# Encoder trunk, opening of layer 0: inputs handed over transposed, norm weight multiplied into the split, root of the mean square applied behind the products

## The chip, the cores and the metric

The kernel runs on one core of one Trainium2 chip. The core has engines that run side by side, each working through its own list in order: TensorE (PE in the profile, with PEld for its weight loads), VectorE (DVE), ScalarE (ACT), GpSimd (POOL) and SyncE (SP, which issues most of the transfers). The metric is the device time of one execution in microseconds (us), lower is better; what counts is the median of several runs.

## The reference, cut to what matters

The program is a two-layer encoder on one sequence of 1024 tokens of width 1024, with 256 memory tokens. Layer 0 has windowed attention, layer 1 a gated linear recurrence; each also has four cross-attention heads into the memory, and ends with a convolutional feed-forward part. What matters here is the opening:

```python
def rmsnorm(x, g):
    y = xf * lax.rsqrt(jnp.mean(xf * xf, axis=-1, keepdims=True) + NORM_EPS)
    return (y * g.astype(F32)).astype(x.dtype)
...
mem_n = rmsnorm(mem, mem_norm_g)
h = x
for layer in range(DEPTH):
    u = rmsnorm(h, norm_g[layer, 0])
    mem_kv = mem_n @ w_mem_kv[layer]
    y = mixer_window_attn(u, mem_kv, a_w_in[slot], ...)    # layer 0
    ...
# in mixer_window_attn
q, k, v, xq = jnp.split(u @ w_in, ...)
q, k = rope(q), rope(k)
s = jnp.einsum(xq, memory keys) * X_HEAD_DIM ** -0.5       # cross-attention
```

A norm is thus a factor for each token (the root) and a factor for each channel (the weight g). The root of a token goes through a product unchanged, since it scales a whole row of the product's input; g does not.

## The kernel before, in words

Products run in three passes on PE for accuracy (`mm3`, lines 80 to 83): each operand is split into a high part `h` in a shortened format and a rest `l`, and high x high, low x high and high x low are added up in one PSUM bank. The split of a tile is two operations: ACT casts `h` (line 86, or line 76 for a weight unit), DVE subtracts for `l` (line 87 or 77). A weight unit (`wunit`, lines 69 to 78) is one transfer by SP into one of four stage buffers, then this split into one of four ring buffers.

`start()` (line 1367) makes the normed, transposed and split inputs. `rows` (line 1374) loads a block of 128 tokens, `norm_T` (lines 107 to 118) sums its squares on ACT (line 100), makes the mean on DVE (line 91), takes the power -0.5 on POOL (line 93: one column, since a token's root is one number for each partition), multiplies by root and weight on DVE (line 112), turns it by eight transposes on PE (line 116) and splits what comes out of PSUM. Two blocks of the memory become `mh`, `ml`; eight blocks of x become `uh`, `ul`.

`memory_kv` (lines 148 to 176) runs right behind the two memory blocks. For each of two layers it makes four key blocks (`km`: 24 products 128x256 each, weights as the stationary side, so that memory tokens lie along the columns) and two value blocks (`vm`: 48 products 128x512, memory tokens on the partitions), and sends them to memory (`kvd`). Key and value blocks all take a bank from one PSUM pool of four (`psb`, tag `pb`). After each key block and each value unit, `step` takes up one more block of x, so the norm of x runs between the products of the memory.

`window()` (line 227) follows: `proj` (line 252) makes query, key and value of a group of heads (24 products 128x384 into a bank `pj`), turns queries and keys by the tables `cos` and `sin` (lines 274 and 275), adds on POOL (276, 277) and splits the values (279, 280). `cross_unit` (line 185) does the cross-attention with the largest score, a scale and an exponential (lines 204 to 209).

The lists of the engines are made by a scheduler ahead of time: it simulates the program with its own costs and writes down for each engine the order in which it got to the instructions. So an edit in the opening can change the order everywhere behind it. Waits between engines are semaphores; an engine whose next instruction waits does nothing else meanwhile.

Of the kernel before, what the change touches and what calls it, by code (L numbers as in the profile page):

```python
# [27 lines left out]
RING = 4  # L28
STAGE = 4

MEM_POOL = 1
QKV_POOL = (0, 2, 2, 2)

XU = [(0, 2), (0, 2), (2, 2), (0, 0)]
# [12 lines left out]
def build(tc, A, out):  # L47
# [12 lines left out]
    up = tc.alloc_tile_pool(name="uT", bufs=1)  # L60

    ident = cp.tile([P, P], F32, name="ident")
    nc.sync.dma_start(ident, A["ident"])
# [81 lines left out]

    kvd = [dram.tile([4, P, 2, 256], F32, name=f"kvd{l}") for l in range(2)]

    def memory_kv(tp, psb, mh, ml, step):

        for l in range(2):  # L150
            km = tp.tile([P, 4, 256], F32, tag="km", bufs=1, name="km")
            vm = tp.tile([P, 2, 512], F32, tag="vm", bufs=1, name="vm")
            for h in range(4):
                wh, wl = wunit(A["wmk"][l, h], eng=pool if 4 * l + h < MEM_POOL else None)
                ps = psb.tile([P, 512], F32, tag="pb", name="pb")
                for k in range(KT):
                    c = slice(k * P, (k + 1) * P)
                    mm3(ps[:, :256], wh[:, c], wl[:, c], mh[:, k, :], ml[:, k, :], k == 0, k == KT - 1)
                act.copy(km[:, h, :], ps[:, :256])
                step()  # L160
            pv = [psb.tile([P, 512], F32, tag="pb", name="pb") for _ in range(2)]
            for u in range(4):
                wh, wl = wunit(A["wmv"][l, u])
                for i in range(2):
                    k = 2 * u + i
                    c = slice(i * 512, (i + 1) * 512)
                    for t in range(2):
                        m = slice(t * P, (t + 1) * P)
                        mm3(pv[t], mh[:, k, m], ml[:, k, m], wh[:, c], wl[:, c], k == 0, k == KT - 1)
                step()  # L170
            for t in range(2):
# [13 lines left out]
    def cross_unit(l, h, b, head, wp, tags, w0, pair):  # L185

        wh, wl, kvh, kvl = head
        ps = tags["pj"][2].tile([P, 512], F32, tag=tags["pj"][0], bufs=tags["pj"][1], name="pj")
        for k in range(KT):
            c = slice(k * P, (k + 1) * P)  # L190
            m = slice(b * 512, (b + 1) * 512)
            mm3(ps, wh[:, c], wl[:, c], uh[:, k, m], ul[:, k, m], k == 0, k == KT - 1)
        xh, xl = pair("x", b)
        with tc.high_priority(AHEAD):
            split(xh, xl, ps)
        p = wp.tile([P, 4, 256], F32, tag="sm", bufs=tags["sm"], name="xp")
# [25 lines left out]
        ot = w0.tile([P, 512], F32, tag=tags.get("xo", "xo"), bufs=1, name="xo")  # L222
        act.copy(ot, po)
        act.dma_start(oT[l][8 + h, :, b * 512:(b + 1) * 512], ot)


    def window():
# [24 lines left out]
        def proj(g):  # L252
# [6 lines left out]
            for b in range(2):  # L259
                rqs = []  # L260
                for tt in range(4):
                    t = 4 * b + tt
                    ps = psq.tile([P, 384], F32, tag="pj", bufs=2, name="pj")
                    for k in range(KT):
                        wh, wl = us[k // 2]
                        c = slice((k % 2) * 384, (k % 2 + 1) * 384)
                        m = slice(t * P, (t + 1) * P)
                        mm3(ps, uh[:, k, m], ul[:, k, m], wh[:, c], wl[:, c], k == 0, k == KT - 1)
                    t1 = ea.tile([P, 320], F32, tag="t1", bufs=1, name="t1")
                    t2 = ea.tile([P, 320], F32, tag="t2", bufs=1, name="t2")  # L270
# [12 lines left out]
                for w in range(3):  # L283
# [1080 lines left out]
        return late  # L1364


    def start():
        psp = tc.alloc_tile_pool(name="mps", bufs=2, space=PSUM, reuse_waits="tile")
        psb = tc.alloc_tile_pool(name="mpb", bufs=4, space=PSUM, reuse_waits="tile")
        tp = tc.alloc_tile_pool(name="mt", bufs=2, reuse_waits="tile")  # L1370
        mh = tp.tile([P, KT, 256], F32R, bufs=1, name="mh")
        ml = tp.tile([P, KT, 256], F32R, bufs=1, name="ml")

        def rows(src, t, g, dh, dl):
            x = tp.tile([P, D], F32, tag="x", bufs=4, name="x")
            nc.sync.dma_start(x, src[t * P:(t + 1) * P, :])
            if not g:
                g.append(grow(tp, *g_src.pop(0)))
            norm_T(tp, psp, x, g[0], dh, dl, t)

        g_src = [(A["mem_norm_g"], "gm"), (A["norm_g"][0, 0:1, :], "g0")]
        gm, g0 = [], []
        for t in range(2):
            rows(A["mem"], t, gm, mh, ml)
        left = list(range(NT))

        def step():
            if left:
                rows(A["x"], left.pop(0), g0, uh, ul)

        memory_kv(tp, psb, mh, ml, step)
        tp.release()
        psb.release()
        psp.release()
# [5 lines left out]
    wo0.finish()  # L1400
    ffn(0, wo0, h2d, True, (0, 1), (0, 1))
    late = hgrn()
    wo1.finish()
# [6 lines left out]
def prepare(i):  # L1410
# [8 lines left out]

    a = {}  # L1420
    a["x"] = c(f["x"].reshape(T, D))
    a["mem"] = c(f["mem"].reshape(256, D))
    a["norm_g"] = c(f["norm_g"])
    a["mem_norm_g"] = c(f["mem_norm_g"].reshape(1, D))
# [64 lines left out]
```

## Time and profile before

| | |
|---|---|
| median of 3 runs | 2690.17 us (2688.71 to 2694.20) |
| profiled execution | 2686.47 us, its span 2684.7 us |
| mean granted clock of TensorE | 0.993 |
| first and last product of the memory | 13.99 and 67.54 us |
| first product of `proj` | 67.77 us |
| output projection of layer 0, first sum on DVE | 495.4 us |

The span runs from the first to the last instruction; 1.8 us of the execution lie outside it. A row of instructions in the profile reads: line, engine, operation, tile written and tiles read, shape, count, then the busy time and the mean of one in ns, the idle time ahead of them and who ended it. Buffer numbers are left out of the names there. Matmuls overlap on PE, so their durations add up to more than they take; the distance between two starts is what one costs.

### The profile page before, as it was taken

The numbers are of one execution on the slowest core, as the hardware profiler recorded it, in microseconds if no ns is written. First come the engines' busy times: TensorE is split into PE (matmuls) and PEld (weight loads), VectorE is DVE, ScalarE is ACT, GpSimd is POOL, SyncE is SP. The second block draws the span as 40 slices with busy tenths as digits, with TensorE's granted clock in tenths as the row PEclk, the third lists the DMA queues.
The fourth block names the chain that finished last, engine by engine and source line by source line (L and its number), as shares of the span: only waits on it lengthen the run. The fifth ranks groups of instructions, "written<-read, shape, count | busy, mean of one in ns | idle before, by whom it ended". The sixth has DMA issues, their size and how long they took to land.

```text
span 2684.7 us, 39333 instructions
## 1 busy us (share of the span) xinstructions
PE 2618.3 (98%) x14496; PEld 2200.0 (82%) x14496; DVE 1827.6 (68%) x3026; ACT 1384.6 (52%) x2530; POOL 469.4 (17%) x520
## 2 busy tenths in 40 slices
PE   8999999999999999999999999999999999999998
PEld 7888897788888887887888888888888788888886
DVE  6587787678656565478778686796757755656456
ACT  6367666645444445455455454545534444444453
POOL 1231110111111100032223132230211111110013
PEclk9999998999999999999999999999999999999999
DMA  7674213557877756674326252102436777774666
GB/s 281 213 166 104 60 28 117 176 183 181 216 199 200 205 165 243 191 241 157 103 84 177 76 120 70 48 29 83 150 119 178 183 202 210 198 205 160 220 196 228
DMA packets 204626, 427.00 MB, mean 159 GB/s; under 512 B 20112, under 2 KB 66576, under 8 KB 198800
## 3 DMA queue, kind: packets, MB, share of 16 engines
q1 hardware_dynamic: 171168, 326.68, 37.5%
q0 software_dynamic: 24544, 90.19, 16.1%
q10 hardware_dynamic: 8720, 7.60, 0.9%
q8 instruction: 114, 1.87, 0.3%
q14 instruction: 80, 0.66, 0.1%
HBM read 331.08 MB, written 117.44 MB: 167 GB/s over the span
## 4 chain that ended last, share of the span: by engine, by line
PE 77%; DVE 13%; ACT 4%; DMA 3%; issue 2%; POOL 1%; SPq 0%; DVEq 0%; ACTq 0%; POOLq 0%
PE X L638 27%; PE V L638 11%; PE pj L81 5%; PE pj L82 5%; PE Y L638 5%; PE pj L83 5%; PE pb L82 3%; PE pb L81 3%; PE pb L83 3%; DVE E L1194 1%; DVE ER L1229 1%; PE pt L338 1%; PE pt L116 1%; DVE wl L87 1%; PE po L1297 1%
## 5 line engine op out<-in xcount | busy, mean ns | idle before, releaser
L87 DVE TENSOR_TENSOR wl<-st,wh 128x1024 fp32r<-128x1024 f32 (+1 forms) x238 | 263.5, 1114 | 325.7 <-ACT wh L86 318.3
L86 ACT CAST wh<-st 128x1024 fp32r<-128x1024 f32 (+1 forms) x238 | 222.5, 937 | 295.2 <-PE X L638 196.2
L81 PE MATMUL pj<-uh,wh 128*128 128x512 f32 x512 | 204.1, 399 | 3.8 <-DVE xl L87 2.5
L638 PE MATMUL X<-wl,wh 128*128 128x512 f32 x528 | 204.8, 390 | 0.3 <-DVE wl L87 0.3
L638 PE MATMUL X<-wh,wl 128*128 128x512 f32 x528 | 204.6, 389 | 0.0
L82 PE MATMUL pj<-ul,wh 128*128 128x512 f32 x512 | 202.5, 396 | 0.1
L83 PE MATMUL pj<-uh,wl 128*128 128x512 f32 x512 | 201.6, 394 | 0.0
L638 PE MATMUL X<-wh 128*128 128x512 f32 x528 | 198.8, 390 | 1.7 <-DVE c L1014 0.9
L81 PE MATMUL pj<-wh,uh 128*128 128x384 f32 (+1 forms) x512 | 190.4, 372 | 4.2 <-DVE gs L1125 3.8
L82 PE MATMUL pj<-wl,uh 128*128 128x384 f32 (+1 forms) x512 | 187.3, 366 | 0.0
L83 PE MATMUL pj<-wh,ul 128*128 128x384 f32 (+1 forms) x512 | 186.8, 366 | 0.0
L77 DVE TENSOR_TENSOR wl<-st,wh 128x1024 fp32r<-128x1024 f32 (+1 forms) x92 | 119.9, 1310 | 28.1 <-ACT wh L76 27.4
L638 PE MATMUL V<-uh,wh 128*128 128x512 f32 x344 | 133.8, 389 | 0.0
L638 PE MATMUL V<-ul,wh 128*128 128x512 f32 x344 | 133.8, 389 | 0.0
L638 PE MATMUL V<-uh,wl 128*128 128x512 f32 x344 | 133.8, 389 | 0.0
L76 ACT CAST wh<-st 128x1024 fp32r<-128x1024 f32 (+1 forms) x99 | 99.9, 1015 | 50.5 <-PE pj L82 27.8
L638 PEld LDWEIGHTS X<-wh 128*128 128x128 f32 x528 | 99.1, 188 | 22.9 <-issue 1.3
L81 PEld LDWEIGHTS pj<-uh,wh 128*128 128x128 f32 x512 | 96.7, 189 | 24.2 <-DVE xl L87 2.9
L638 PEld LDWEIGHTS X<-wl,wh 128*128 128x128 f32 x528 | 99.1, 188 | 21.2 <-DVE wl L87 0.7
L638 PEld LDWEIGHTS X<-wh,wl 128*128 128x128 f32 x528 | 99.1, 188 | 20.8
L83 PEld LDWEIGHTS pj<-uh,wl 128*128 128x128 f32 x512 | 96.8, 189 | 19.2
L980 POOL TENSOR_TENSOR c<-c,g 128x512 f32<-128x512 f32 x24 | 43.4, 1828 | 393.8 <-PE X L638 162.8
(372 smaller groups left out, 7257.4 us busy)
## 6 DMA issues: line engine op xcount, KB each, us to landing
st<-hid SPq DMA_DIRECT2D x154, 256.0 KB, 3.1
st<-in_ffw_dram SPq DMA_DIRECT2D x108, 256.0 KB, 3.2
w2s<-in_ffw_dram POOLq DMA_DIRECT2D x24, 1024.0 KB, 7.9
st<-in_ffw_dram SPq DMA_DIRECT2D x46, 512.0 KB, 4.1
hid<-tt SPq DMA_DIRECT2D x88, 256.0 KB, 4.6
st<-w2s SPq DMA_DIRECT2D x88, 256.0 KB, 2.8
sx<-in_ffw_dram SPq DMA_DIRECT2D x84, 256.0 KB, 3.9
sy<-in_ffw_dram SPq DMA_DIRECT2D x42, 512.0 KB, 6.2
```

The source lines that it names most:

```text
L76: act.copy(h[:, :n], raw)
L77: (eng or dve).tensor_tensor(l[:, :n], raw, h[:, :n].bitcast(F32), op=ALU.subtract)
L81: pe.matmul(o, ah, bh, start=first, stop=False)
L82: pe.matmul(o, ah, bl, start=False, stop=False)
L83: pe.matmul(o, al, bh, start=False, stop=last)
L86: act.copy(h, src)
L87: dve.tensor_tensor(l, src, h.bitcast(F32), op=ALU.subtract)
L116: pe.transpose(ps[:, k, :], u[:, (4 * b + k) * P:(4 * b + k + 1) * P], ident)
L338: pe.transpose(tp[:, j, :], sm[:, j, c * P:(c + 1) * P], ident)
L638: pe.matmul(o, x, y, start=new, stop=e, skip_group_check=not first)
L980: pool.tensor_tensor(y[q][:, t, :], y[q][:, t, :], g3[:, c], op=ALU.mult)
L1194: dve.tensor_tensor_scan(B[:, rev], smask, a_[:, rev], 0.0, op0=ALU.mult, op1=ALU.add)
```

## The change

The host hands over x and mem already transposed (`xT`, `memT`) and the two norm weights turned so that a channel's weight lies on the channel's partition (`gT`). The kernel no longer transposes. With channels on partitions the weight is a factor for each partition, so ACT's cast takes it as its scale, and DVE's subtraction multiplies by it too (`scaled`). The root stays out of the split operands and is applied behind the products:

- memory keys: the eviction of a key block becomes a multiplication on DVE by `rsb`, the roots of the 256 memory tokens laid out on every partition;
- memory values: the eviction takes `rsm`, a token's root on its partition, as a scale;
- queries and keys of layer 0: the tables `cos` and `sin` are multiplied by `rs0`; values take it as a scale, both in the cast and in the subtraction;
- cross-attention of layer 0: the scale of the exponential and of the largest score become `xsc`, the root times the old constant.

The squares are summed over channels, which now lie on partitions, so PE does it by products with a tile of ones. For `rsb` ACT squares the memory, POOL adds the eight slices down to one, a product with ones gives the sum on every partition, DVE makes the mean, and POOL takes the power of a tile of 128x256. For x, ACT squares each slab and POOL adds it to `acc`; eight products with ones at the end give `rs0`. The first weight unit's subtraction moves from POOL to DVE, memT is loaded by ACT's queue, and `ident` is loaded later. The pool `x0`, which holds `rs0` and `xsc`, stays until the output projection is done.

```diff
-MEM_POOL = 1
...
-    def memory_kv(tp, psb, mh, ml, step):
+    def memory_kv(tp, psb, mh, ml, rsb, rsm, begin, step):
...
-                wh, wl = wunit(A["wmk"][l, h], eng=pool if 4 * l + h < MEM_POOL else None)
+                wh, wl = wunit(A["wmk"][l, h])
...
-                act.copy(km[:, h, :], ps[:, :256])
+                if l == h == 0:
+                    begin()
+                dve.tensor_tensor(km[:, h, :], ps[:, :256], rsb, op=ALU.mult)
                 step()
...
-                act.copy(vm[:, t, :], pv[t])
+                act.activation(vm[:, t, :], pv[t], AF.Copy, scale=rsm[:, t:t + 1])
...
-            dve.tensor_scalar_mul(st["nm"][:, e], st["nm"][:, e], -XSCALE)
+            if l == 0:
+                dve.tensor_tensor(st["nm"][:, e], st["nm"][:, e], xsc[:, 1, 4 * b + 2 * i:4 * b + 2 * i + 2], op=ALU.mult)
...
-                               scale=XSCALE, accum_out=st["su"][:, q:q + 1])
+                               scale=xsc[:, 0, 4 * b + q:4 * b + q + 1] if l == 0 else XSCALE, accum_out=st["su"][:, q:q + 1])
...
+        dve.tensor_tensor(cos, cos, bc(rs0.unsqueeze(2), [P, NT, 32]), op=ALU.mult)
+        s2 = sin.rearrange("p t a b -> p t (a b)")
+        dve.tensor_tensor(s2, s2, bc(rs0.unsqueeze(2), [P, NT, 64]), op=ALU.mult)
...
-                    act.copy(v[:, t, :64], ps[:, 320:])
-                    dve.tensor_tensor(v[:, t, 64:], ps[:, 320:], v[:, t, :64].bitcast(F32), op=ALU.subtract)
+                    act.activation(v[:, t, :64], ps[:, 320:], AF.Copy, scale=rs0[:, t:t + 1])
+                    dve.scalar_tensor_tensor(v[:, t, 64:], ps[:, 320:], rs0[:, t:t + 1], v[:, t, :64].bitcast(F32),
+                                             op0=ALU.mult, op1=ALU.subtract)
...
     def start():
...
+        for k in range(0, KT, 2):
+            act.dma_start(mT[:, k:k + 2], A["memT"][:, k:k + 2])
+
+        def scaled(h, l, raw, g):
+            act.activation(h, raw, AF.Identity, scale=g)
+            dve.scalar_tensor_tensor(l, raw, g, h.bitcast(F32), op0=ALU.mult, op1=ALU.subtract)
+
+        for k in range(KT):
+            scaled(mh[:, k], ml[:, k], mT[:, k], gT[:, 0, k:k + 1])
...
+        def memory_rstd():
+            for k in (0, 4):
+                act.activation(msq[:, k:k + 4], mT[:, k:k + 4], AF.Square)
+            for n in (4, 2, 1):
+                pool.tensor_tensor(msq[:, :n], msq[:, :n], msq[:, n:2 * n], op=ALU.add)
+            pb = pss.tile([P, 256], F32, name="pbc")
+            pe.matmul(pb, ones, msq[:, 0], start=True, stop=True)
+            ms = tp.tile([P, 256], F32, name="mms")
+            dve.tensor_scalar(ms, pb, 1.0 / D, EPS, op0=ALU.mult, op1=ALU.add)
+            with tc.high_priority(AHEAD):
+                pool.tensor_tensor(rsb, ms, bc(nhalf[:, 0:1], [P, 256]), op=ALU.pow)
+            pc = pss.tile([P, 2], F32, name="pcc")
...
         def step():
...
+            raw = tp.tile([P, T], F32, tag="x", bufs=4, name="x")
+            nc.sync.dma_start(raw, A["xT"][k])
+            scaled(uh[:, k], ul[:, k], raw, gT[:, 1, k:k + 1])
+            if k == 0:
+                act.activation(acc, raw, AF.Square)
+            else:
+                sq = tp.tile([P, T], F32, tag="sq", bufs=2, name="sq")
+                act.activation(sq, raw, AF.Square)
+                pool.tensor_tensor(acc, acc, sq, op=ALU.add)
...
+        for t in range(NT):
+            pe.matmul(pt[:, t:t + 1], acc[:, t * P:(t + 1) * P], ones[:, 0:1], start=True, stop=True)
+        ms = tp.tile([P, NT], F32, name="xms")
+        dve.tensor_scalar(ms, pt, 1.0 / D, EPS, op0=ALU.mult, op1=ALU.add)
+        pool.tensor_tensor(rs0, ms, nhalf, op=ALU.pow)
+        dve.tensor_scalar_mul(xsc[:, 0], rs0, XSCALE)
+        dve.tensor_scalar_mul(xsc[:, 1], rs0, -XSCALE)
```

The edit also moves instructions on every engine. Three places matter; the rows are the engines' lists as the scheduler wrote them, with buffer numbers. First PE, where the last of the first four key blocks ends and the first value blocks begin (`pb_323` and `pb_253` are the fourth key block, `pb_373`, `pb_374` and `pb_286`, `pb_287` the value blocks). Before:

```order
L81 MATMUL pb_323<-mh_93,wh_317 128x256
L82 MATMUL pb_323<-ml_94,wh_317 128x256
L83 MATMUL pb_323<-mh_93,wl_318 128x256
L81 MATMUL pb_373<-wh_375,mh_93 128x512
L81 MATMUL pb_374<-wh_375,mh_93 128x512
L82 MATMUL pb_373<-wl_376,mh_93 128x512
```

And now:

```order
L1409 MATMUL pbc_166<-msq_124,ones_99 128x256
L1416 MATMUL pcc_171<-ones_99,msq_124 128x1 x2
L80 MATMUL pb_253<-ml_103,wh_247 128x256
L81 MATMUL pb_253<-mh_102,wl_248 128x256
L79 MATMUL pb_253<-mh_102,wh_247 128x256
L80 MATMUL pb_253<-ml_103,wh_247 128x256
L81 MATMUL pb_253<-mh_102,wl_248 128x256
L79 MATMUL pb_286<-wh_288,mh_102 128x512
L80 MATMUL pb_286<-wl_289,mh_102 128x512
L81 MATMUL pb_286<-wh_288,ml_103 128x512
```

The products with ones stand inside the fourth key block, and the value blocks still follow it; they take the fifth and sixth bank of a pool of four.

Second the evictions of the key blocks, which free those banks (`km`). Before, on ACT, they stood each among the work that follows its block (`nu` is a block of x squared, `uh` its cast, `wh` a weight unit's cast):

```order
L159 COPY km_145<-pb_211 128x256
L76 CAST wh_375<-st_377 128x1024
L86 CAST uh_78<-pt_247 128x4x128
L159 COPY km_145<-pb_267 128x256
L86 CAST uh_78<-pt_254 128x4x128
L100 ACTIVATE nu_352,nss_351<-x_349 128x1024
```

Now they are on DVE:

```order
L1411 TENSOR_SCALAR mms_168<-pbc_166 128x256
L1418 TENSOR_SCALAR mm2_174<-pcc_171 128x2
L1394 SCALAR_TENSOR_TENSOR ul_78<-x_331,gT_97,uh_77 128x1024
L75 TENSOR_TENSOR wl_289<-st_290,wh_288 128x1024
L75 TENSOR_TENSOR wl_314<-st_315,wh_313 128x1024
L75 TENSOR_TENSOR wl_339<-st_340,wh_338 128x1024
L1394 SCALAR_TENSOR_TENSOR ul_78<-x_356,gT_97,uh_77 128x1024
L75 TENSOR_TENSOR wl_364<-st_365,wh_363 128x1024
L1394 SCALAR_TENSOR_TENSOR ul_78<-x_381,gT_97,uh_77 128x1024
L1394 SCALAR_TENSOR_TENSOR ul_78<-x_427,gT_97,uh_77 128x1024
L1394 SCALAR_TENSOR_TENSOR ul_78<-x_466,gT_97,uh_77 128x1024
L159 TENSOR_TENSOR km_128<-pb_136,rsb_125 128x256
```

The first eviction stands behind four weight subtractions and five slab splits that come after the mean `mms`, and three more evictions follow it in a row.

Third POOL, where `rsb` is made. Before, its list in the opening held the powers of one column and one weight subtraction:

```order
L93 TENSOR_TENSOR nrs_104<-nms_102,nhalf_76 128x1
L93 TENSOR_TENSOR nrs_128<-nms_126,nhalf_76 128x1
L77 TENSOR_TENSOR wl_148<-st_149,wh_147 128x1024
L93 TENSOR_TENSOR nrs_188<-nms_186,nhalf_76 128x1
L93 TENSOR_TENSOR nrs_244<-nms_242,nhalf_76 128x1
```

Now:

```order
L1407 TENSOR_TENSOR msq_124<-msq_124 128x1024
L1407 TENSOR_TENSOR msq_124<-msq_124 128x512
L1407 TENSOR_TENSOR msq_124<-msq_124 128x256
L1436 TENSOR_TENSOR acc_127<-acc_127,sq_283 128x1024
L1436 TENSOR_TENSOR acc_127<-acc_127,sq_310 128x1024
L1413 TENSOR_TENSOR rsb_125<-mms_168,nhalf_75 128x256
L1419 TENSOR_TENSOR rsm_126<-mm2_174,nhalf_75 128x2
L1436 TENSOR_TENSOR acc_127<-acc_127,sq_335 128x1024
L1436 TENSOR_TENSOR acc_127<-acc_127,sq_360 128x1024
```

Ten powers of one column are gone; the power for `rsb` has 256 columns and stands behind two of the seven additions to `acc`, with five behind it.

More of the change, by code (lines that the diff above doesn't have):

```diff
@@ L62, in build @@
     ident = cp.tile([P, P], F32, name="ident")
-    nc.sync.dma_start(ident, A["ident"])
     nhalf = cp.tile([P, 8], F32, name="nhalf")
@@ L204, in cross_unit @@
             dve.reduce_max(st["nm"][:, e], s, axis=AX.X)
-            dve.tensor_scalar_mul(st["nm"][:, e], st["nm"][:, e], -XSCALE)
+            if l == 0:
+                dve.tensor_tensor(st["nm"][:, e], st["nm"][:, e], xsc[:, 1, 4 * b + 2 * i:4 * b + 2 * i + 2], op=ALU.mult)
+            else:
+                dve.tensor_scalar_mul(st["nm"][:, e], st["nm"][:, e], -XSCALE)
             for j in range(2):
@@ L1364, in hgrn @@
         return late
+    x0 = tc.alloc_tile_pool(name="x0", bufs=1, reuse_waits="tile")
+    rs0 = x0.tile([P, NT], F32, name="rs0")
+    xsc = x0.tile([P, 2, NT], F32, name="xsc")
     def start():
-        psp = tc.alloc_tile_pool(name="mps", bufs=2, space=PSUM, reuse_waits="tile")
+        pss = tc.alloc_tile_pool(name="mps", bufs=1, space=PSUM, reuse_waits="tile")
         psb = tc.alloc_tile_pool(name="mpb", bufs=4, space=PSUM, reuse_waits="tile")
-        tp = tc.alloc_tile_pool(name="mt", bufs=2, reuse_waits="tile")
@@ L1371, in start @@
[L1371 to L1382, printed above, removed]
@@ L1383, in start @@
-        for t in range(2):
-            rows(A["mem"], t, gm, mh, ml)
-        left = list(range(NT))
-        def step():
-            if left:
-                rows(A["x"], left.pop(0), g0, uh, ul)
-        memory_kv(tp, psb, mh, ml, step)
+        tp = tc.alloc_tile_pool(name="mt", bufs=1, reuse_waits="tile")
+        gT = tp.tile([P, 2, KT], F32, name="gT")
+        nc.sync.dma_start(gT, A["gT"])
+        ones = tp.tile([P, P], F32, name="ones")
+        pool.memset(ones, 1.0)
+        mT = tp.tile([P, KT, 256], F32, name="mT")
@@ new lines, in start @@
+        mh = tp.tile([P, KT, 256], F32R, name="mh")
+        ml = tp.tile([P, KT, 256], F32R, name="ml")
+        for k in range(0, KT, 2):
[5 more added lines that the diff above has]
+            scaled(mh[:, k], ml[:, k], mT[:, k], gT[:, 0, k:k + 1])
+        msq = tp.tile([P, KT, 256], F32, name="msq")
@@ new lines, in start @@
+        rsb = tp.tile([P, 256], F32, name="rsb")
+        rsm = tp.tile([P, 2], F32, name="rsm")
+        def memory_rstd():
[10 more added lines that the diff above has]
+            pc = pss.tile([P, 2], F32, name="pcc")
+            for t in range(2):
+                pe.matmul(pc[:, t:t + 1], msq[:, 0, t * P:(t + 1) * P], ones[:, 0:1], start=True, stop=True)
+            ms2 = tp.tile([P, 2], F32, name="mm2")
+            dve.tensor_scalar(ms2, pc, 1.0 / D, EPS, op0=ALU.mult, op1=ALU.add)
+            pool.tensor_tensor(rsm, ms2, nhalf[:, :2], op=ALU.pow)
@@ new lines, in start @@
+        acc = tp.tile([P, T], F32, name="acc")
+        left = [None, None] + list(range(KT))
+        def step():
+            k = left.pop(0) if left else None
+            if k is None:
+                return
+            raw = tp.tile([P, T], F32, tag="x", bufs=4, name="x")
[3 more added lines that the diff above has]
+                act.activation(acc, raw, AF.Square)
+            else:
+                sq = tp.tile([P, T], F32, tag="sq", bufs=2, name="sq")
+                act.activation(sq, raw, AF.Square)
+                pool.tensor_tensor(acc, acc, sq, op=ALU.add)
@@ new lines, in start @@
+        memory_kv(tp, psb, mh, ml, rsb, rsm, memory_rstd, step)
+        nc.sync.dma_start(ident, A["ident"])
+        pt = pss.tile([P, NT], F32, name="ptt")
+        for t in range(NT):
[4 more added lines that the diff above has]
+        dve.tensor_scalar_mul(xsc[:, 0], rs0, XSCALE)
@@ L1392, in start @@
+        dve.tensor_scalar_mul(xsc[:, 1], rs0, -XSCALE)
         tp.release()
         psb.release()
-        psp.release()
+        pss.release()
     wo0 = WOut(0, A["x"], "wout0", list(range(NT)))
@@ L1400, in build @@
     wo0.finish()
+    x0.release()
     ffn(0, wo0, h2d, True, (0, 1), (0, 1))
@@ L1421, in prepare @@
     a["x"] = c(f["x"].reshape(T, D))
-    a["mem"] = c(f["mem"].reshape(256, D))
+    turned = lambda x: c(x.T.reshape(KT, P, x.shape[0]))
+    a["xT"] = turned(f["x"].reshape(T, D))
+    a["memT"] = c(turned(f["mem"].reshape(256, D)).transpose(1, 0, 2))
+    a["gT"] = np.stack([c(f["mem_norm_g"].reshape(KT, P).T), c(f["norm_g"][0, 0].reshape(KT, P).T)], axis=1)
     a["norm_g"] = c(f["norm_g"])
-    a["mem_norm_g"] = c(f["mem_norm_g"].reshape(1, D))
     wm = f["w_mem_kv"]
```

## The prediction

> **What bounds the kernel now.** I read the page first, for who is busy.
>
> ```profile
> span 2684.7 us, 39333 instructions
> PE 2618.3 (98%) x14496; PEld 2200.0 (82%) x14496; DVE 1827.6 (68%) x3026; ACT 1384.6 (52%) x2530; POOL 469.4 (17%) x520
> PE 77%; DVE 13%; ACT 4%; DMA 3%; issue 2%; POOL 1%; SPq 0%; DVEq 0%; ACTq 0%; POOLq 0%
> ```
>
> PE works 98% of the span, and the chain that ended last lies on it for 77%. So an edit pays only by taking instructions from PE or by shortening a time in which PE stands still; one that makes PE stand still costs that time in full. The edit touches the opening, so next come the table of stretches (length, then busy time of PE, weight loads, DVE, ACT, POOL, granted clock, DMA share, GB/s) and the timeline of the opening (start, duration).
>
> ```profile
> 0.00:10.00 10.00, 1.52 (x7) 1.52 (x8) 1.59 (x3) 3.95 (x6) 1.17 (x7) 1.00 0.72 270
> 10.00:20.00 10.00, 8.10 (x47) 7.19 (x46) 8.11 (x11) 8.52 (x14) 4.84 (x4) 1.00 1.03 414
> 14.00:67.80 53.80, 53.65 (x354) 49.22 (x354) 42.28 (x51) 37.53 (x60) 6.18 (x8) 1.00 0.77 272
> ```
>
> ```profile
> 5.08 1.06 ACT L100 ACTIVATE nu<-x 128x1024 f32<-128x1024 f32 x1 [3.06 <-DMA x<-in_mem_dram]
> ...
> 13.99 0.58 PE L81 MATMUL pb<-mh,wh 128*128 128x256 f32 x1
> ...
> 15.10 0.41 PE L83 MATMUL pb<-mh,wl 128*128 128x256 f32 x1
> ...
> 15.31 0.41 PE L81 MATMUL pb<-mh,wh 128*128 128x256 f32 x1
> ...
> 17.64 0.60 PE L116 MATMUL pt<-ident,nu 128*128 128x128 f32 x4
> ...
> 18.00 0.36 PE L82 MATMUL pb<-ml,wh 128*128 128x256 f32 x1
> ...
> 54.82 0.28 PE L82 MATMUL pb<-ml,wh 128*128 128x256 f32 x1
> 54.94 0.28 PE L83 MATMUL pb<-mh,wl 128*128 128x256 f32 x1
> 55.06 0.40 PE L81 MATMUL pb<-wh,mh 128*128 128x512 f32 x1
> 55.29 0.40 PE L82 MATMUL pb<-wl,mh 128*128 128x512 f32 x1
> ...
> 67.77 0.33 PE L81 MATMUL pj<-wh,uh 128*128 128x384 f32 x1
> 67.94 0.34 PE L82 MATMUL pj<-wl,uh 128*128 128x384 f32 x1
> ```
>
> PE's first product is at 13.99, the first query/key/value product (pj) at 67.77, and between them PE is busy without a break. Starts count, not durations, since matmuls overlap: a 128x256 product takes 0.12 us, a 128x512 one 0.23, a pj one 0.17, four transposes 0.36; the first products, from cold, take 0.21 in place of 0.12.
>
> **The change, part by part.** All before pj: the sum is the new start of pj against 67.77.
>
> *Earlier start.* The first product no longer waits for squares, a root and transposes (8.48 to 13.99), only for a quarter of memT, the first weight unit and its cast. memT (1 MB, ACT's queue) and that unit (0.5 MB, SP's) run together; at 270 GB/s 1.5 MB are in at 5.6, and a cast takes 1.05. Estimate 6.8 (5.5 to 9): **-7.2 us**.
>
> *Transposes.* The 16 of the memory lie in the opening; the 64 of x go: 16 groups of four at 0.36, **-5.8**. The stretch holds 192 products at 0.12 and 96 at 0.227, 44.8, plus 1.6 for the cold start and 5.8: 52.2 of 53.8. The 1.6 left are gaps around the transposes: **-1.6**.
>
> *Ones products* (three before the values, eight before pj, true float32, a form that this stretch lacks): at least 0.12 each, 1.3; at most four times that, 5.3. Most have one column, so near the low end: **+1.6**.
>
> *The wait for rsb.* The key blocks are now evicted by a multiplication with rsb. The pool has four banks: four key blocks fill them, and the first value block (pb_286 in the order) needs the bank of the first, so PE cannot pass the 96th product until rsb exists. PE is there at 6.8 + 96 x 0.12 + 1.6 + 0.6 = 20.5. When does rsb come? POOL makes it, behind the square sums and two additions to acc.
>
> ```profile
> L77 POOL TENSOR_TENSOR wl<-st,wh 128x1024 fp32r<-128x1024 f32 x1 | 2.5, 2531 | 1.0 <-ACT wh L76 1.0
> L1237 POOL TENSOR_TENSOR E<-EP,q 128x256 f32<-128x256 f32 x64 | 51.2, 800 | 289.9 <-DVE EP L1230 218.1 <-ACT gs L1101 18.8 <-issue 14.2
> L76 ACT CAST wh<-st 128x1024 fp32r<-128x1024 f32 x17 | 17.6, 1051 | 4.7 <-DMA st<-in_wmk_dram 2.4 <-PE pb L82 2.3
> L100 ACT ACTIVATE nu<-x 128x1024 f32<-128x1024 f32 x10 | 10.7, 1069 | 5.1 <-DMA x<-in_mem_dram 5.1
> L159 ACT COPY km<-pb 128x256 f32<-128x256 f32 x8 | 3.0, 374 | 1.4 <-PE pb L83 1.4
> L77 DVE TENSOR_TENSOR wl<-st,wh 128x1024 fp32r<-128x1024 f32 x16 | 19.3, 1222 | 3.0 <-ACT wh L76 2.8
> L112 DVE SCALAR_TENSOR_TENSOR nu<-x,nrs,g 128x1024 f32<-128x1024 f32 x8 | 10.3, 1282 | 3.0 <-POOL nrs L93 3.0
> ```
>
> The last addition ahead of rsb needs the square of x's third slab. By the order ACT does up to it 8 slices of 128x256 (0.37), 2 squares of the memory, 4 casts, 3 scaled slabs and 3 squares (1.06 each): 3.0 + 12 x 1.06 = 15.7. The memory's first half was in at 5.08 before; a quarter should be in at 4.5: 20.2. An addition of 128x1024 takes 2.5 on POOL: rsb begins at 22.7, with some interference 24 (22.5 to 26). Its own time is the question.
>
> ```profile
> L93 POOL TENSOR_TENSOR nrs<-nms,nhalf x34: 538/548/3790, 6.6 to 2043.7; 128x1 f32<-128x1 f32 x34
> L93 POOL TENSOR_TENSOR ors<-oms,nhalf x16: 1006/1036/1146, 1374.0 to 1937.9; 128x4 f32<-128x4 f32 x16
> ```
>
> ```profile
> 17.76 1.23 DVE L77 TENSOR_TENSOR wl<-st,wh 128x1024 fp32r<-128x1024 f32 x1
> 17.80 1.59 POOL L93 TENSOR_TENSOR nrs<-nms,nhalf 128x1 f32<-128x1 f32 x1 [3.53 <-DVE nms L91]
> ```
>
> The power of one column takes 548 ns (min/median/max stand in the row), of four 1036: (1036 - 548) / 3 = 163 ns a column more. rsb is a power of 256 columns: 0.55 + 255 x 0.163 = 42.1 us. Low bound: an ordinary POOL operation of that size, 0.80. I take the slope, since both of its rows are of this very operation, while the 0.80 is a product's. The second pair shows interference: a power that began beside a DVE subtraction on two SBUF tiles took 1.59 and ended 0.4 behind it. During rsb DVE has 4 subtractions and 5 slab splits of that kind, 4 x 1.22 + 5 x 1.28 = 11.3: between 0 and 11.3 more; I take 5. rsb is there at 24 + 47 = 71. PE stands from 20.5: **+50.5**, and 0.4 for the eviction.
>
> [...]
>
> *Reheating.* After a stall PE is slow:
>
> ```profile
> 76.00:79.20 3.20, 0.64 (x4) 0.20 (x2) 2.60 (x6) 0.78 (x2) 1.72 (x3) 0.93 0.04 13
> 79.20:82.20 3.00, 3.00 (x10) 3.00 (x11) 1.01 (x3) 0.21 (x1) 2.26 (x4) 0.50 0.80 281
> ```
>
> Behind 2.6 us idle the clock was 0.50 for 3 us: **+1.6**.
>
> *Costed at nothing.* Behind rsb POOL has five additions (12.7 us), and squares with two buffers hold ACT until about the third; the next casts follow some 10 us after rsb, their subtraction at 11.8, and PE first has 48 value products (10.9, and 1.6 cold): covered by about 1 us; gone if the additions run at 3.5, then up to 3. rs0 for x, another power (8 columns, 0.55 + 7 x 0.163 = 1.7), and the scaled tables (two DVE operations, about 1.2 together) follow the ones products while PE fills two pj banks (48 x 0.17 = 8); without that cover 3.4. DVE takes key evictions (8 x 0.37) from ACT and one subtraction from POOL, ACT squares of the same 1.07, and both idle during the wait. v's scale, xsc and the value evictions ride on instructions that were there.
>
> Sum: -7.2 - 5.8 - 1.6 + 1.6 + 50.5 + 0.4 + 1.6 = **+39.5 us**; pj begins at 107. In the window stage the order of DVE and PE changes in detail, and there stalls and cold spells lie close together:
>
> ```profile
> 410.00:420.00 10.00, 8.56 (x28) 6.24 (x28) 9.19 (x34) 8.49 (x28) 0.00 (x0) 0.50 0.47 141
> ```
>
> One such spell more or less is 5 us of PE time; I take 0, bounds -8 and +8. From the output projection on, the order is the same.
>
> **The rivals.** *First, the power costs what a product costs* (the other side). With 0.8 in place of 47 PE stands 4.8 us: 39.5 - 50.5 + 4.8 = -6.2. For it: 0.8 is well measured, and two widths make a thin slope. Against: both widths are powers, and the sixteen of four columns all lie between 1006 and 1146 ns. It decides below 7.5 us (29 ns a column), where gain and wait cancel. 2684 on the median.
>
> *Second, the loop over columns overlaps*, and a long power costs less than half the slope: 10 to 20 us, so 39.5 - 47 + (13 to 23), +5.5 to +15.5: 2696 to 2706. Four columns would be too few to show it.
>
> *Third, DVE keeps POOL out fully*, the additions run late and the backlog bites: rsb starts at 26 and takes 53.4, 3 for the backlog: 39.5 + 2 + 6.4 + 3 = +51, 2741. For it: the 1.59 us row; against: a power reads little and computes much.
>
> **How the numbers follow.** The profiled execution took 2686.47, 1.8 outside its span; the median of the runs is 3.7 higher. 2686.5 + 39.5 = 2726.0 on the first basis, 2690.2 + 39.5 = 2730 on the second, which I forecast. The slope (from half of it to all, with some interference) gets 0.78, the first rival 0.09, the second 0.07, the third 0.06. Low end: half the slope, 21, and 3 for interference, 39.5 - 47 + 24 = +16.5, 2706; high end: the third rival and part of the window's bound, 2747. What a measurement can tell from no change is about 0.2%, 5.4 us: faster 0.07 (most of the first rival), same 0.04, slower 0.89.
>
> **What would show it.** Right: one POOL power 128x256 of some 40 us; PE idle in that time, released by DVE's km; first product near 7, first pj near 107; the half clock behind the wait; no transposes before pj. Wrong: a power under 8 us, or value products that run before rsb because the banks are not those I think; then pj begins near 61. If pj is right and the end is not, the window stage took or gave the rest.

## The result, and the profile after

| | before | after |
|---|---|---|
| median of the runs | 2690.73 us | 2724.11 us (2722.07 to 2727.99, 4 runs) |
| ratio | 1 | 1.0125 [1.0109, 1.0141] |
| profiled execution, and its span | 2686.47, 2684.7 us | 2727.99, 2726.2 us |
| first product | 13.99 us | 7.36 us |
| first pj product | 67.77 us | 106.67 us |

The change costs 33.4 us by the medians. The page of the changed kernel first: the busy time of each engine, and the chain that ended last, by engine.

```profile
PE 2616.8 (96%) x14438; PEld 2195.9 (81%) x14438; DVE 1831.4 (67%) x3018; ACT 1388.2 (51%) x2508; POOL 532.5 (20%) x523
PE 79%; DVE 10%; ACT 3%; DMA 3%; POOL 3%; issue 2%; SPq 0%; DVEq 0%; ACTq 0%; POOLq 0%
```

PE works 1.5 us less than before, in a span that is 41.5 us longer: the time was not spent on work, PE stood. POOL works 63 us more and has gone from 1% to 3% of the chain. The table of stretches says when (length, then busy time of PE, weight loads, DVE, ACT and POOL with their instructions, granted clock, DMA share, GB/s), and the table of PE's waits up to 80 us says for whom (total, times, longest).

```profile
0.00:30.00 30.00, 14.67 (x102) 13.91 (x102) 22.25 (x20) 24.70 (x30) 16.61 (x12) 0.92 0.84 306
30.00:60.00 30.00, 0.00 (x0) 0.00 (x0) 7.62 (x7) 2.65 (x3) 30.00 (x1) 0.50 0.23 82
60.00:80.00 20.00, 10.52 (x38) 8.45 (x39) 2.51 (x5) 5.07 (x5) 19.68 (x7) 0.67 0.08 26
```

```profile
PE pb L79 <- DVE km L159: 46.1, 1, 46.1
PE pb L79 <- ACT wh L74: 7.4, 1, 7.4
PE pb L81 <- DVE wl L75: 1.4, 2, 0.9
```

From 30 to 60 us PE executes nothing, and POOL executes one instruction all the while. One wait holds 46.1 us; the 7.4 is the time up to the first product. The wait is put down to `km`, DVE's eviction of a key block, but that instruction was itself waiting. POOL's timeline (start, duration, operation) names it:

```profile
13.60 6.58 POOL L1407 TENSOR_TENSOR msq<-msq 128x1024 f32<-128x1024 f32 x3 [12.62 <-ACT msq L1405]
20.14 6.65 POOL L1436 TENSOR_TENSOR acc<-acc,sq 128x1024 f32<-128x1024 f32 x2
26.75 42.13 POOL L1413 TENSOR_TENSOR rsb<-mms,nhalf 128x256 f32<-128x256 f32 x1
68.86 0.70 POOL L1419 TENSOR_TENSOR rsm<-mm,nhalf 128x2 f32<-128x2 f32 x1
69.54 13.14 POOL L1436 TENSOR_TENSOR acc<-acc,sq 128x1024 f32<-128x1024 f32 x5
107.72 1.65 POOL L1445 TENSOR_TENSOR rs<-xms,nhalf 128x8 f32<-128x8 f32 x1 [25.04 <-DVE xms L1444]
```

The root of 256 columns runs from 26.75 to 68.88. PE's timeline shows what that does to the products:

```profile
23.11 0.28 PE L81 MATMUL pb<-mh,wl 128*128 128x256 f32 x1
69.48 0.76 PE L79 MATMUL pb<-wh,mh 128*128 128x512 f32 x1 [46.09 <-DVE km L159]
...
73.03 0.40 PE L81 MATMUL pb<-wh,ml 128*128 128x512 f32 x1
73.27 0.39 PE L79 MATMUL pb<-wh,mh 128*128 128x512 f32 x1
```

The last key product starts at 23.11, the first value product at 69.48, 0.6 us behind the root. Nine products start between 69.48 and 73.03, most of them 0.43 us apart, at a granted clock of 0.50, and from there they are 0.23 to 0.24 apart: the slow restart.

### The profile page after: what moved, and what is told of

Its sections match the earlier page's. It is cut to its first block, busy times and chain, and to the rows that moved or that the text cites. A ratio compares the mean times of both kernels' runs of the same rounds, so it can differ in the third digit from the quotient of the medians.

```text
span 2726.2 us, 39176 instructions
## 1 busy us (share of the span) xinstructions
PE 2616.8 (96%) x14438; PEld 2195.9 (81%) x14438; DVE 1831.4 (67%) x3018; ACT 1388.2 (51%) x2508; POOL 532.5 (20%) x523
## 4 chain that ended last, share of the span: by engine, by line
PE 79%; DVE 10%; ACT 3%; DMA 3%; POOL 3%; issue 2%; SPq 0%; DVEq 0%; ACTq 0%; POOLq 0%
PE X L645 27%; PE V L645 11%; PE pj L79 6%; PE pj L80 6%; PE pj L81 6%; PE Y L645 5%; PE pb L79 3%; PE pb L80 3%; PE pb L81 3%; POOL rsb L1413 2%; PE pt L345 1%; DVE E L1201 1%; PE po L1304 1%; DVE ER L1236 1%; DVE wl L85 1%
```

## The experiments

Each kernel is the changed one with the edit shown, but for the last three repeats and where another is named. Ratios are to the kernel before, on the same chip, with their intervals. "pj" is the start of the first pj product; "window stage" is the time from it to DVE's first sum of the output projection.

### Is it the power? (e1_mult, e2_half, e3_banks)

```diff
# e1_mult
-pool.tensor_tensor(rsb, ms, bc(nhalf[:, 0:1], [P, 256]), op=ALU.pow)
+pool.tensor_tensor(rsb, ms, bc(nhalf[:, 0:1], [P, 256]), op=ALU.mult)
# e2_half
+pool.tensor_tensor(rsb[:, :P], ms[:, :P], bc(nhalf[:, 0:1], [P, P]), op=ALU.pow)
+pool.tensor_tensor(rsb[:, P:], ms[:, P:], bc(nhalf[:, 0:1], [P, P]), op=ALU.mult)
# e3_banks
-psb = tc.alloc_tile_pool(name="mpb", bufs=4, ...)
+psb = tc.alloc_tile_pool(name="mpb", bufs=5, ...)
```

Expected of e1_mult:

> The changed kernel with one operation swapped: rsb is the product of the mean square and -0.5 in place of its power -0.5, same engine, same 128x256 shape, same place in POOL's list (the keys are then scaled by the wrong factor). Theory (the 42 us are the power's own time, and PE's wait is nothing else): rsb takes about 1 us, PE's wait before the first value block shrinks from 46 to about 5 us, first pj product near 66, total about 41 us below the changed kernel: 2683 (2678 to 2690). Rival (the loss lies in the new order of the lists or in interference between POOL and DVE): the total stays above 2705.

Expected of e2_half:

> Power on the first 128 of rsb's columns, a product on the other 128 (second half of the keys wrongly scaled). Theory (163 ns for each column, no fixed part worth mentioning): the power takes 0.55 + 127 x 0.163 = 21.3 us, the wait falls by about 20, total 2704 (2700 to 2709). Rival (a fixed cost, such as code being loaded for a wide power): the power stays above 30 us and the total above 2712.

Expected of e3_banks:

> Five PSUM banks for the key and value blocks in place of four, nothing else. Theory (PE waits for a bank, not for rsb as such): the first value block, 24 products of 0.23 us, now runs inside the wait, PE's idle time falls from 46 to about 40.5, and the total by about 5.5: 2718.5 (2715 to 2722). Rival (PE waits for something else that rsb releases): no change, 2724.

| | median | ratio | root or product, us | PE's wait for km | pj |
|---|---|---|---|---|---|
| changed kernel | 2724.11 | 1.0125 [1.0109, 1.0141] | 42.13 | 46.1 | 106.67 |
| e3_banks | 2720.38 | 1.0114 [1.0098, 1.0129] | 42.13 | 31.6 | 101.31 |
| e2_half | 2704.88 | 1.0060 [1.0045, 1.0075] | 21.73 + 0.39 | 25.9 | 87.79 |
| e1_mult | 2692.92 | 1.0016 [1.0006, 1.0025] | 1.60 | 6.5 | 75.98 |

Two groups on POOL of e2_half up to 80 us (busy time, mean ns of one), then PE's waits of e3_banks up to 80 us:

```profile
L1413 POOL TENSOR_TENSOR rsb<-mms,nhalf 128x128 f32<-128x128 f32 x1 | 21.7, 21731 | 0.0
L1414 POOL TENSOR_TENSOR rsb<-mms,nhalf 128x128 f32<-128x128 f32 x1 | 0.4, 389 | 0.0
```

```profile
PE pb L79 <- DVE km L159: 31.6, 1, 31.6
...
PE pb L80 <- DVE wl L75: 5.9, 1, 5.9
```

Line 1413 is the power of 128 columns, line 1414 a product of the same size. The power goes by columns: 128 more cost 42.13 - 21.73 = 20.4 us, 159 ns each, and PE's wait shrinks by 46.1 - 25.9 = 20.2 with it. The cause of the main loss is shown. The fifth bank shows the way by which it acts: PE runs one value block further before it stands. The wait falls by 14.5, but 5.9 come back as a wait for `wl`, since that block's products ran ahead of their weight splits; the same end, at the root, stands behind them. PE stood 37.5 us in these two waits where 40.5 were expected, pj moved by 5.4, about the block's 24 products at 0.23, and the median lies in the expected range.

e1_mult missed its expectation by 10 us, and by more than its interval. The product took 1.6 us and the wait for it was 6.5, as forecast; but pj came at 75.98, ten later than expected and eight later than in the kernel before. Its waits, the groups of DVE up to 80 us, and one of POOL:

```profile
PE pb L79 <- DVE km L159: 6.5, 1, 6.5
PE pb L81 <- DVE wl L75: 2.7, 2, 2.3
PE pb L80 <- DVE wl L75: 2.7, 1, 2.7
```

```profile
L75 DVE TENSOR_TENSOR wl<-st,wh 128x1024 fp32r<-128x1024 f32 x16 | 26.6, 1683 | 4.0 <-ACT wh L74 4.0
L1394 DVE SCALAR_TENSOR_TENSOR ul<-x,gT,uh 128x1024 fp32r<-128x1024 f32 x8 | 20.0, 2532 | 0.6 <-ACT uh L1393 0.6
```

```profile
L1436 POOL TENSOR_TENSOR acc<-acc,sq 128x1024 f32<-128x1024 f32 x7 | 22.0, 3137 | 0.4
```

PE waits 5.4 us for weight splits. The weight splits (`wl`) take 1683 ns and the slab splits (`ul`) 2532, where such operations took 1222 and 1282 before; POOL's additions take 3137 ns, against 13.14 / 5 = 2.63 us for the five that ran in the changed kernel while DVE did little. So a second cost seems to be there, hidden under the power's: POOL's additions and DVE's operations slow each other. The next two runs test it.

### The second cost (e6_late, e7_noadds)

e6_late takes the root's long shape away, and keeps what is computed. ACT copies the key blocks out unscaled, so banks come free at once. The memory's root is taken with tokens on partitions (128x2), spread by a product of ones with a diagonal matrix, and multiplied onto a layer's keys in SBUF before they are stored. It also replaces two of the memory's three additions on POOL by eight one-column products, gives `km` a second buffer and loads `ident` earlier, by ACT's queue; these are not in the cut below. e7_noadds is e6_late without x's seven additions, so that the root of x comes from the first slab alone.

```diff
# e6_late
-dve.tensor_tensor(km[:, h, :], ps[:, :256], rsb, op=ALU.mult)
+act.copy(km[:, h, :], ps[:, :256])
...
+dve.tensor_tensor(km, km, bc(rsb.unsqueeze(1), [P, 4, 256]), op=ALU.mult)
...
-pool.tensor_tensor(rsb, ms, bc(nhalf[:, 0:1], [P, 256]), op=ALU.pow)
...
+pool.tensor_tensor(rsm, ms2, nhalf[:, :2], op=ALU.pow)
...
+for t in range(2):
+    dve.tensor_scalar_mul(dg[:, t * P:(t + 1) * P], ident, rsm[:, t:t + 1])
...
+pe.matmul(pb, ones, dg, start=True, stop=True)
+act.copy(rsb, pb)
...
# e7_noadds, beyond e6_late
-pool.tensor_tensor(acc, acc, sq, op=ALU.add)
```

Expected of e6_late:

> Same result as the reference, by another way: ACT copies the key blocks out of PSUM unscaled, as in the kernel before, and DVE multiplies all four by the roots later, in SBUF, ahead of the transfer; the roots of the memory are a power of two columns, spread over the partitions by a product of ones with a diagonal; eight one-column products replace two of POOL's three additions. Theory (with the wait out of PE's way the rest of the change is worth its transposes and its earlier start): first pj product near 59.5, 8 us before that of the kernel before, total 2682 (2678 to 2687). Rival (the slabs' squares and additions hold ACT and POOL back, so that PE starves): first pj not before 66, total 2689 or more.

Expected of e7_noadds:

> The kernel with the late scaling of the keys (e6_late), with the seven additions of x's squares on POOL left out, so that layer 0's root comes from the first slab alone. Theory (POOL's additions slow DVE's operations on two SBUF tiles, which make PE wait for weight and slab splits): DVE's slab splits fall from 2.25 us to about 1.27 each, weight splits from 1.49 to 1.23, PE's 10 us of waits for them go, first pj product near 62 in place of 75, total about 13 below e6_late: 2676 (2671 to 2681). Rival (transfers, or ACT with its squares, set the pace of the opening): pj stays above 71 and the total above 2685.

Measured: e6_late 2689.19, ratio 1.0001 [0.9992, 1.0010], pj 75.23; e7_noadds 2681.18, ratio 0.9966 [0.9953, 0.9979], pj 60.34. In e6_late no wait for a root is left, yet pj is where e1_mult had it, and both numbers are where its rival put them. PE's waits and the groups of DVE and POOL, first of e6_late, then of e7_noadds:

```profile
PE pb L80 <- DVE wl L75: 5.5, 4, 2.8
PE pb L81 <- DVE wl L75: 4.5, 2, 4.0
```

```profile
L75 DVE TENSOR_TENSOR wl<-st,wh 128x1024 fp32r<-128x1024 f32 x16 | 23.7, 1493 | 8.0 <-ACT wh L74 8.0
L1396 DVE SCALAR_TENSOR_TENSOR ul<-x,gT,uh 128x1024 fp32r<-128x1024 f32 x8 | 17.9, 2253 | 0.6 <-ACT uh L1395 0.6
```

```profile
L1439 POOL TENSOR_TENSOR acc<-acc,sq 128x1024 f32<-128x1024 f32 x7 | 21.5, 3078 | 6.3 <-ACT sq L1438 6.1
```

```profile
PE pb L79 <- ACT wh L74: 8.6, 1, 8.6
...
PE pb L81 <- DVE wl L75: 0.5, 1, 0.5
```

```profile
L75 DVE TENSOR_TENSOR wl<-st,wh 128x1024 fp32r<-128x1024 f32 x16 | 19.3, 1222 | 6.8 <-ACT wh L74 6.8
L1396 DVE SCALAR_TENSOR_TENSOR ul<-x,gT,uh 128x1024 fp32r<-128x1024 f32 x8 | 11.4, 1459 | 0.6 <-ACT uh L1395 0.6
```

Without the additions DVE's weight splits are back at 1222 ns and the slab splits at 1.27 to 1.28 us, but for one of 2.75 beside the addition of the memory's squares that is left. PE waits 0.5 us for `wl` in place of 10.0, and pj comes 14.9 us sooner. That is more than the wait; the clock differed too: in e6_late, where PE waited in pieces, the granted clock was 0.96 up to 30 us and 0.87 from there to 60, in e7_noadds 1.00 in both, an estimated 30 x 0.04 + 30 x 0.13 = 5.1 us. ACT waited nowhere for POOL in e6_late's opening, so it was not the squares that held PE. The end gains 8.0, since e7_noadds' window stage took 424.2 us and e6_late's 420.8, and what follows differs by 3 more; so its median lies 0.2 above the expected range. So the additions are the second cause: seven operations on an engine with little to do took away the whole gain of the missing transposes.

### Two versions without that cost (e8_rows, e9_mem)

e8_rows starts from e6_late and has no additions on POOL at all: x and the memory are loaded a second time, token by token, and ACT sums the squares of a row as it goes (a sum that ACT makes beside its output). DVE copies the key blocks out. e9_mem keeps the kernel before for x and changes only the memory's half, scaled late.

```diff
# e8_rows
-sq = tp.tile([P, T], F32, tag="sq", bufs=2, name="sq")
-act.activation(sq, raw, AF.Square)
-pool.tensor_tensor(acc, acc, sq, op=ALU.add)
...
+nc.sync.dma_start(xr, src[t * P:(t + 1) * P, :])
+sumsq(tp, xr, ss[:, t:t + 1], junk)
# e9_mem
-for t in range(2):
-    rows(A["mem"], t, gm, mh, ml)
...
+for k in range(KT):
+    scaled(mh[:, k], ml[:, k], mT[:, k], gT[:, 0, k:k + 1])
```

Expected of e8_rows:

> Same result as the reference. As e6_late, but the squares are summed by ACT alone: the blocks of 128 tokens of mem and x are loaded a second time in their old layout (5 MB more), and one square with a sum on ACT for each block gives the token's sum on its partition, so that neither POOL's additions nor products with ones are needed for the sums. DVE copies the key blocks out of PSUM. Theory (with POOL quiet the change is worth its earlier start and its transposes): first pj product near 61, total 2676 (2671 to 2682). Rival (5 MB more of transfers, or ACT with ten squares, become the bound of the opening): pj at 68 or later, total 2684 or more.

Expected of e9_mem:

> Half of the change, same result as the reference: only the memory is handed over transposed, with the late scaling of the keys; x is normed, transposed on PE and split as in the kernel before. One addition on POOL is left. Theory (what the memory half is worth is the earlier first product, less one-column products; x's transposes stay): first product near 8.5, DVE's splits undisturbed, first pj product near 64.5, 3 us before that of the kernel before; total 2686 if the order of the window stage is as before, 2680 if its new order comes along. Rival (the earlier start is lost again since the splits of the weights or the transfers cannot feed PE): pj at 67.5 or later, total 2689 or more.

Measured: e8_rows 2681.73, ratio 0.9972 [0.9961, 0.9984], pj 63.79; e9_mem 2685.36, ratio 0.9978 [0.9969, 0.9988], pj 68.24. Both beat both kernels. e8_rows took 6 us more than expected, at the upper edge of its range; PE's waits up to 80 us and two stretches of its table say why a part of it:

```profile
PE pb L79 <- ACT wh L74: 11.8, 3, 8.8
...
PE pb L80 <- DVE wl L75: 1.2, 1, 1.2
PE pb L81 <- DVE wl L75: 1.0, 1, 1.0
```

```profile
0.00:30.00 30.00, 19.74 (x123) 17.91 (x124) 20.93 (x29) 22.43 (x30) 1.15 (x7) 1.00 0.93 361
30.00:60.00 30.00, 26.23 (x152) 23.20 (x151) 18.57 (x19) 20.51 (x26) 0.00 (x0) 0.94 0.97 356
```

With the ten row loads (5 MB more) the DMA engines are 93% busy up to 30 us and 97% from there to 60, against 92 and 75% in e7_noadds. Behind the first product PE waits 5.2 us (3.0 for casts of weights, 2.2 for their splits), against 0.5 in e7_noadds. Whether rows loaded later would bring pj nearer to e7_noadds' 60.3 was not tried. e9_mem came out at the higher of its two values, but pj where its rival had it. Its gain isn't in the opening: the first product is 5.2 us sooner (8.79), but pj is no earlier than before (68.24 against 67.77), and the window stage (next) holds what it won. What ate the 5.2 us was not taken apart; 2.7 of it are waits for splits.

### The window stage (r1_before, r2_before, r3_after)

These are the two kernels unchanged, once more each for a further trace (the one before twice).

Expected of r1_before:

> The kernel before once more, for a second trace of its window stage (first product of window() to the first sum of the first output projection: 427.7 us in its trace shown, 422.9 in the changed kernel's). Theory: the changed order of the stage is worth the 4.8 us, so this trace gives 427.0 to 428.5 again. Rival: the length of the stage moves by some us from one execution to the next, whatever the order, so this trace gives a time more than 1.5 us away, towards 424.

Expected of r2_before:

> The same kernel a third time: under the theory 427.0 to 428.5 once more; under the rival a third time, somewhere from 423 to 428.

Expected of r3_after:

> The changed kernel once more: under the theory the window stage takes 422.0 to 423.8, under the rival anything from 420 to 427. Both expect the root over 256 columns to take 42.1 us again, TensorE to wait 46 for it, and window()'s first product at 106 to 107.5.

The first pj product, and the first sum of the output projection, of r1_before, r2_before and r3_after:

```profile
67.63 0.33 PE L81 MATMUL pj<-wh,uh 128*128 128x384 f32 x1
495.73 0.69 DVE L466 TENSOR_TENSOR y<-pb,part 128x512 f32<-128x512 f32 x1
```

```profile
68.13 0.33 PE L81 MATMUL pj<-wh,uh 128*128 128x384 f32 x1
497.87 0.69 DVE L466 TENSOR_TENSOR y<-pb,part 128x512 f32<-128x512 f32 x1 [0.93 <-PE pb L83]
```

```profile
107.33 0.42 PE L79 MATMUL pj<-wh,uh 128*128 128x384 f32 x1
530.99 0.68 DVE L473 TENSOR_TENSOR y<-pb,part 128x512 f32<-128x512 f32 x1
```

Before, the stage takes 428.1 and 429.7 us here and 427.7 in the first trace; after, 423.7 here and 423.0 in the first. The second repeat lies 1.2 above the theory's upper bound, on the side away from the rival: the length moves by some 2 us, and the two sets stay 4 apart. On the means, 428.5 and 423.3, the stage gave back 5.2 us. Two of PE's waits in the stage went with it, first before, then after:

```profile
PE ptq L286 <- POOL rq L276: 2.6, 2, 2.1
...
PE pj L81 <- DVE xl L87: 2.5, 1, 2.5
```

```profile
PE pj L79 <- DVE xl L85: 0.7, 1, 0.7
...
PE ptq L293 <- POOL rq L282: 0.3, 1, 0.3
```

These two alone mislead, for others grew: all of PE's waits in the stage add up to 21.3, 23.4 and 24.9 us in the three traces before and to 18.4 and 19.0 after. The mean granted clock of the stage was 0.96 in the first trace before and 0.98 in the first after. Why the two waits went, and why the clock was higher, stays open. It isn't the scaled tables or values alone: e9_mem has neither, and its stage took 424.3. Nor is it the waits alone: e9_mem's add up to 22.8. All nine traces of kernels that take the memory transposed gave 420.8 to 424.3. In r3_after the root took 42.1 us again, PE waited 46.1 for it, and pj came at 107.33, as both theories expected.

## Why the prediction was right, point by point

| step | forecast | measured |
|---|---|---|
| first product | 6.8 us | 7.36 |
| PE has issued the 96 key products | 20.5 | 23.39 (69.48 - 46.09) |
| rsb begins | 24 | 26.75 |
| its own time, and interference | 42.1 + 5 | 42.13 in all, some 1.1 of it interference |
| rsb is there | 71 | 68.88 |
| wait | 50.5 | 46.09 |
| ones products | 1.6 | about 2.5 (0.8 inside the fourth key block, 0.43 of that for the one of 256 columns, against 0.12 for a key product of that size; 1.7 before pj) |
| reheating | 1.6 | 1.7 (69.48 to 73.27 for 9 products of 0.23) |
| first pj | 107 | 106.67 |
| window stage | 0 (-8 to +8) | -5.2 |
| the whole, on the medians | +39.5 | +33.4 |

- **The power's price** was the step that mattered, and it held: the slope of two rows of 1 and 4 columns (163 ns) gave 42.1 us for 256 columns, and the trace shows 42.13, against the first and the second rival. e2_half shows that the line is straight in between. That the two agree to 0.03 is luck: the power's own time was about 41.0, 160 ns a column, and 1.1 of waiting made up the rest (next point). The product of the same size took 1.60 us in e1_mult, beside DVE.
- **Interference on the power** was the term that was mis-sized: 5 us forecast, about 1.1 measured. Single rows of POOL and then of DVE show where it lies, beside two additions and then beside the power that began at 26.75:

```profile
20.14 3.36 POOL L1436 TENSOR_TENSOR acc<-acc,sq 128x1024 f32<-128x1024 f32 x1
23.58 3.22 POOL L1436 TENSOR_TENSOR acc<-acc,sq 128x1024 f32<-128x1024 f32 x1
```

```profile
14.59 2.75 DVE L1394 SCALAR_TENSOR_TENSOR ul<-x,gT,uh 128x1024 fp32r<-128x1024 f32 x1 [0.61 <-ACT uh L1393]
...
21.18 3.40 DVE L1394 SCALAR_TENSOR_TENSOR ul<-x,gT,uh 128x1024 fp32r<-128x1024 f32 x1
...
24.91 2.97 DVE L1394 SCALAR_TENSOR_TENSOR ul<-x,gT,uh 128x1024 fp32r<-128x1024 f32 x1
27.80 1.63 DVE L75 TENSOR_TENSOR wl<-st,wh 128x1024 fp32r<-128x1024 f32 x1
...
33.95 3.67 DVE L1394 SCALAR_TENSOR_TENSOR ul<-x,gT,uh 128x1024 fp32r<-128x1024 f32 x3
```

  The two engines took turns. Each of the five splits that ran beside POOL's additions took 1.75 to 3.40 us and ended 1.07 to 1.09 behind the addition beside it: 21.18 + 3.40 = 24.58, and the first addition ended at 23.50. The second addition ended 2.2 behind that split in turn. The power waited in the same way, once: it began at 26.75, and the split beside it ended at 27.88. Its length fits: 0.70 and 1.65 us for two and eight columns, with DVE idle, make 40.9 for 256 columns and 20.7 for 128, and the two long powers took 1.2 and 1.1 more. Powers of one, two and eight columns lost as much when they began beside DVE: 1.59 for 0.55 in the kernel before, 1.69 for 0.70 in e1_mult, 2.62 for 1.65 in e7_noadds. But the power did not hold DVE up for its length. The first split behind its start took 1.63, the later ones 1.21 to 1.27, which is their own time. The row of 1.59 us that the prediction read shows this one wait; spreading it over all of DVE's splits was the error. The third rival did the same: its later start came (26.75 for its 26), its 11.3 us of interference did not.
- **The wait** came out 4.4 smaller than forecast. The root was there 2.1 sooner, for interference was small and a later start ate part of that; PE stopped 2.9 later; and 0.6 passed between root and first value product. Of the 2.9, 0.6 is the later first product and 1.4 the wait for `wl`; most of the rest is ones products and cold products. rsb began 2.75 later than forecast because POOL was not free. The square that it was to wait for was done at 20.44, as forecast (20.2), but POOL worked without a break from 13.60 on the memory's three additions (6.58) and two of x (6.65, 3.3 each and not 2.5). That pj came within 0.6 of its forecast is luck in part: the root was 2.1 sooner, and from the restart to pj PE took 37.2 us where the forecast's terms leave 35.9.
- **The four banks** were read rightly: PE stood exactly between key and value products, and a fifth bank moved the place.
- **Costed at nothing** was wrong in its reason, though it cost nothing here. I wrote that the additions are covered, at most 3 us if they ran at 3.5. In the changed kernel two of the seven additions met splits ahead of the power. Then the power held POOL for 42 us, in which DVE made the rest of the slabs' splits in their own time. The five additions behind it met only the weight splits from 78.91 on, and PE did not wait for those. So the power itself hid this cost. Where it is gone that cover goes with it, and the cost is the 14.9 us of pj that e7_noadds gives back against e6_late.
- For the same reason the **first rival** was priced wrongly. A power as cheap as a product would not have given 2684: e1_mult, which is that rival, ran 2692.92. (Its sum also has a slip of half a microsecond: a root there at 24.8 leaves 4.3 us of wait behind 20.5, not 4.8.) The point of decision, 7.5 us, was wrong: at 1.6 us the kernel was already no faster, 1.0016 [1.0006, 1.0025].
- **The window stage** gave 5.2 us back where I took 0. That is the miss of 6 in the whole: 106.67 - 67.77 = 38.9 for pj, less 5.2, is 33.7, against 33.4 on the medians. It lies within the bounds given, but no step of the prediction foresaw its sign. Of the profiled executions alone (+41.5) the rest is the part behind the stage: it took 2189.3 us in the first trace of the kernel before and 2196.6 in the changed one's, and 2191.4, 2194.4 and 2189.1 in the repeats, so that it differs between executions of one kernel as much.

## What to carry to other kernels

A root taken on POOL cost by its columns (0.70 us for 2, 42.13 for 256), so it belongs where the tokens lie on partitions: 2 columns and a product of ones with a diagonal matrix replace 256. A factor that is late should be applied where nobody waits for the buffer, on a copy in SBUF, not in the instruction that frees a PSUM bank. And work that looks free on an idle POOL has to be priced with what it does to DVE beside it: seven additions of 128x1024 cost the opening more (14.9 us of pj) than sixty-four transposes on PE (5.8 in the prediction's count).

## What the runs showed of the hardware

- A power on POOL over 128 partitions took 0.55 us for 1 column, 0.70 for 2, 1.65 for 8, 21.73 for 128 and 42.13 for 256: some 160 ns a column, with a base of about 0.4 (the two long ones with 1.1 of waiting for DVE in them). The product of 128 columns took 0.39.
- POOL's two-input additions and DVE's operations on two SBUF tiles took turns: beside each other a split ended about 1.1 us behind the addition, and an addition of 128x1024 2.2 behind the split. So an addition of 128x1024 went from 2.4 us (2.63 in the mean of the five behind the power, the last of which met splits) to between 3.1 and 3.4, DVE's splits from 1.22 (weights) and 1.28 (slabs) to as much as 3.4. The 42 us power shows this at its start alone: it waited 1.1 us, the split behind its start took 0.4 longer, and the rest took their own 1.21 to 1.27. Why a power of 42 us held DVE up no longer than that was not shown.
- One DVE operation that read PSUM beside an addition, the 128x256 `mms`, took 0.41 us; the key evictions of that size took 0.42 in the mean.
- After 46 us without work PE ran nine 128x512 products, most of them 0.43 us apart, before it was back at 0.23 to 0.24; the granted clock was 0.50 from 69.48 to 73.03, as it was from 30 to 60 us.
